# Half of each grouped-query pair's maxima one stretch earlier, in a two-layer hybrid attention kernel

## Chip, cores and metric

One core of one Trainium2 chip runs the whole kernel. The metric is the time of one execution in device microseconds (us). TensorE (PE in the profile) does the matmuls, with its weight loads listed apart (PEld); VectorE (DVE), ScalarE (ACT) and GpSimd (POOL) do the elementwise work; SyncE (SP) issues the transfers. TensorE writes its results to PSUM.

## What is computed

Two layers over 1024 latent tokens with 256 context tokens in front. In each layer one projection feeds three groups of heads: six heads of neighbourhood attention (a window of 8 x 16 grid positions and all context keys, with a learned bias), a bidirectional gated linear attention, and six query heads of grouped-query attention over all 1280 keys. Then an output projection, a residual with layer norm, and a gated feed-forward layer. The two softmax attentions are what the change touches:

```
# neighbourhood: scores of the window with a bias, and of the context, in one softmax
s_lat = q_r @ k_s * scale + bias          # outside the window: -inf
s_ctx = q_r @ k_ctx * scale
p = softmax(concat([s_lat, s_ctx]))
# grouped query: all latent and context keys in one softmax
s = q_blk @ keys * d ** -0.5
o = softmax(s) @ vals
```

Layer 0 also computes the outputs of the context tokens (10 blocks of 128 queries); the last layer needs only the latent ones (8 blocks).

## The kernel before

**Pairs and two stages.** Heads are worked on in pairs, two heads side by side in 64 rows each. `PAIRS = (0, 3, 1, 4, 2, 5)`: pairs 0, 1, 2 are neighbourhood pairs, 3, 4, 5 grouped-query pairs. Each pair has two stages. The first (`stage_a`: `na_a`, `ga_a`) finds the largest score of each query, which the softmax subtracts. The second (`stage_b`: `na_b`, `ga_b`) computes the scores again, keys by queries, with the maximum subtracted inside the matmul; then the exponential (ScalarE), the products with the values (TensorE, L950 and L1011) and the sums of the exponentials (GpSimd, L1046 and L1006). The text calls the first stage a pair's **maxima** and the time of a pair's second stage its **stretch**; the six stretches of a layer follow each other in the order of `PAIRS`.

**The maxima.** In `ga_a` (L923) each step is one matmul per head of a 128-query block against 512 or 256 keys (`raw_scores`, L483, tile `gs`) into a two-bank PSUM tile with tag "m", of which there is one buffer, and a VectorE reduction of that tile (L934, into tile `m`). A block of latent queries takes three steps (512, 512, 256 keys), a context block one. In `na_a` (L899) a block takes a step for the context keys (tile `sctx`, reduced at L907) and one for the window (tile `slat`, with two bias-and-maximum instructions, L917), through the same "m" buffer. At the end `max_rows` (L445) transposes the maxima by matmuls (tile `nmT`, L458). With that last part, a grouped-query pair has 27 steps in layer 0 and 25 in the last layer, a neighbourhood pair 19 and 17.

**The second stages.** `ga_b` has 39 places at which it pauses: a block of scores (L475, tile `sT`, two buffers, L945) or a value product (`weigh`, tile `gav`), in turn. `na_b` has 22 places: four blocks of scores over the context keys, their value products (tile `nav`), then eight groups of window scores, each with a bias addition on VectorE (L1023, tile `ptl`), the exponential, and a value product two groups later.

**What sets the order.** Everything is unrolled; each engine works through its own instructions in order. The loop at L1114 takes one place of the current pair's second stage, then some steps of the next pair's maxima, and so on. In a neighbourhood stretch the 27 (25) steps of the following grouped-query pair start after the second place and are spread evenly to the 19th, more than one and a half a place; in a grouped-query stretch the 19 (17) steps of the following neighbourhood pair start after the 12th place and run to the 36th. `in_turn` (L467) chains the matmuls of scores, raw scores and value products in just this written order, so TensorE runs them as written. Loads of a pair's keys, queries and biases are issued on SP's queue by `load` (L868), one pair ahead at least, and wait for free tiles in a pool of 31. The tails of the pair before (`tail`, L1066: normalisation, tile `rb`, through the same "m" buffer) use the first two or three places. The line that spreads the steps:

```
while done < min(na, na * (n - skip) // (places - 3 - skip)):
    next(a, 0)
    done += 1
```

Of the kernel before, what the change touches and what calls it, by code (L numbers as in the profile page):

```python
# [1 line left out]

# [50 lines left out]
def body(ctx: ExitStack, tc, xT, cT, w_ada, w_in, nbias, wa2, w_out, w_fi, w_fo, vecs, cc, consts, ropes, gmask, out):  # L53
# [18 lines left out]
    def slot(dt=F32, name="sl"):  # L72
        return slots.tile([P, NT], dt, tag="s", name=name)
# [239 lines left out]
    def run(g):  # L313
        for _ in g:
            pass
# [117 lines left out]
    def gate(ins, after):  # L433

        if after is not None:
            tc.add_manual_dep(ins.ins, after.ins.name, NOSYNC, reason="buffers in order of use")
        return ins
# [67 lines left out]
    PAIRS = (0, 3, 1, 4, 2, 5)  # L505
# [18 lines left out]
    for l in range(NL):  # L524
# [54 lines left out]
        NBQ = NG  # L579
        A = [slots.tile([P, 10, 2, 64], F32, tag="s", name=f"A{i}") for i in range(2)]  # L580

        def a_mm(p, ga, gb, xk_, X):

            ps = banks2(ps_s, "s", "aps")
            in_order([pe.matmul(ps[64 * c:64 * c + 64, hh, (g - ga) * 64:(g - ga + 1) * 64],
                                lhsT=xk_[32 * (2 * p + hh):32 * (2 * p + hh) + 32, P * g + 64 * c:P * g + 64 * c + 64],
                                rhs=X[32 * (2 * p + hh):32 * (2 * p + hh) + 32, P * g + 64 * c:P * g + 64 * c + 64],
                                start=True, stop=True)
                      for g in range(ga, gb) for c in range(2) for hh in range(2)])
            return (A[p][:, ga:gb].rearrange("p g h t -> p h g t"),  # L590
                    ps[:, :, :(gb - ga) * 64].rearrange("p h (g t) -> p h g t", t=64), gb - ga)

        abanks = [(p, g, min(g + 8, NG)) for g in range(0, NG, 8) for p in range(2)]
        for p, ga, gb in abanks:
            dst, src, n = a_mm(p, ga, gb, gk, gq)
# [6 lines left out]
        for lev in range(6):  # L602
# [8 lines left out]
            for p, ga, gb in abanks:  # L611
                dst, src, n = a_mm(p, ga, gb, xk_, X)
# [224 lines left out]
        def gla_split(pr):  # L837
            O = o_gl[pr]
            a, b = slot(F32R, "oh"), slot(F32R, "ol")
            oh_all[3 + pr], ol_all[3 + pr] = a, b  # L840

            def nat(t):
                return t[:, 0:SEQ].rearrange("p (g r c) -> p r g c", g=8, c=8)

            src = O[:, 0:SEQ].rearrange("p (r g c) -> p r g c", g=8, c=8)
            for r0 in (0, 8):
                sl = slice(r0, r0 + 8)
                act.copy(nat(a)[:, sl], src[:, sl])
                pool.tensor_tensor(out=nat(b)[:, sl], in0=src[:, sl], in1=f(nat(a)[:, sl]), op=ALU.subtract)
                yield  # L850
            if not last:
                act.copy(a[:, SEQ:NT], O[:, SEQ:NT])
                pool.tensor_tensor(out=b[:, SEQ:NT], in0=O[:, SEQ:NT], in1=f(a[:, SEQ:NT]), op=ALU.subtract)
# [5 lines left out]
        def opens(i):  # L859
            return last_b.get(PAIRS[max(0, PAIRS.index(i) - 2)]) if PAIRS.index(i) > 1 else None  # L860

        def load_hl(i, n, after, name):
            ts = [slot(F32R, f"{name}{a}") for a in "hl"]
            for a, t in enumerate(ts):
                gate(nc.sync.dma_start(f(t[:, :n]), sp[l][i][a, :, :n]), after)
            return ts

        def load(i):  # L868
            if i > 5 or i in loaded:
                return  # L870
            loaded.add(i)
            after = opens(i)
            if i < 3:
                kk = load_hl(S_NK + i, NT, after, "K")
                qq = load_hl(S_NQ + i, NQ, after, "Q")

                bs = [slot(F32, f"B{e}") for e in range(3)]
                for v in range(2):
                    for t, c, n, x in ((bs[v], 0, 384, 0), (bs[v], 768, 256, 384), (bs[2], 512 * v, 256, 640)):
                        gate(nc.sync.dma_start(t[:, c:c + 2 * n].rearrange("p (e n) -> p e n", e=2),  # L880
                                               nbias[l, 2 * i:2 * i + 2, v, :, x:x + n].rearrange("e p n -> p e n")), after)
            else:
                if not gkv:
                    gkv.extend(load_hl(S_GK, NT, after, "K"))
                kk, bs = gkv, None
                qq = load_hl(S_GQ + i - 3, NQ, after, "Q")
            heads[i] = [kk, qq, None, bs]
# [193 lines left out]
        def stage_a(i):  # L1081
            return (na_a if i < 3 else ga_a)(i)

        def stage_b(i):
            return (na_b if i < 3 else ga_b)(i)
# [25 lines left out]

        tails += [gla_split(pr) for pr in range(2)]
        sb = {"n": 0, "t": ps_s.tile([P, 2, 2, 512], F32, tag="s4", name="sT", bufs=1)}
        for x, i in enumerate(PAIRS):  # L1114
            nxt = PAIRS[x + 1] if x < 5 else None
            if nxt is not None:
                load(nxt)
            if i >= 3 and x < 4:
                load(PAIRS[x + 2])
            b, a = stage_b(i), stage_a(nxt) if nxt is not None else iter(())  # L1120
            live, tails = tails, []

            places, na, skip = (22, NBQ + 17, 2) if i < 3 else (39, NBQ + 9, 12)
            n = done = 0
            while next(b, 0) is None:
                live = [g for g in live if next(g, 0) is None]
                n += 1
# [3 lines that stand above are left out]
            run(a)  # L1131
            for g in live:
                run(g)
# [213 lines left out]
```

## Time and profile before

| | |
|---|---|
| median of 3 runs | 3759.79 us (3759.14 to 3766.27) |
| the profiled execution | 3766.09 us, span 3764.3 us |
| mean granted TensorE clock | 0.940 |
| TensorE matmuls, busy | 3468.6 us (92% of the span) |
| VectorE, ScalarE, GpSimd, busy | 1650.0, 920.1, 1240.3 us |
| grouped-query maxima: TensorE matmuls (L483, `gs`) | 300 instructions, 90.6 us |
| grouped-query maxima: VectorE reductions (L934) | 150 instructions, 154.7 us |

How to read it: a group's row gives its line, engine, operation, the tile that it writes and those that it reads, the shapes and the count; behind the first bar its busy time and the mean of one in nanoseconds; behind the second the idle time of its engine just before it and what ended most of that. In a row of the stage windows the first number after the stretch is its length, then for each engine the busy time and the number of instructions, and then the TensorE clock that was granted (1 is full speed), the busy share of the DMA engines and the bytes moved. A row of the timeline has the start, the duration of what is merged in the row, engine, line, operation, tiles, count, and in brackets the idle time before it with its releaser.

### The profile page before, as it was taken

The numbers are of one execution on the slowest core, as the hardware profiler recorded it, in microseconds if no ns is written. First come the engines' busy times: TensorE is split into PE (matmuls) and PEld (weight loads), VectorE is DVE, ScalarE is ACT, GpSimd is POOL, SyncE is SP. The second block draws the span as 40 slices with busy tenths as digits, with TensorE's granted clock in tenths as the row PEclk, the third lists the DMA queues.
The fourth block names the chain that finished last, engine by engine and source line by source line (L and its number), as shares of the span: only waits on it lengthen the run. The fifth ranks groups of instructions, "written<-read, shape, count | busy, mean of one in ns | idle before, by whom it ended". The sixth has DMA issues, their size and how long they took to land. (4 is left out here: it accounts for less than half of the span.)

```text
span 3764.3 us, 49308 instructions
## 1 busy us (share of the span) xinstructions
PE 3468.6 (92%) x20832; PEld 2557.0 (68%) x20832; DVE 1650.0 (44%) x2475; ACT 920.1 (24%) x1365; POOL 1240.3 (33%) x747
## 2 busy tenths in 40 slices
PE   6698988788999999999999869998879999999998
PEld 3587873333668888888876658774335688888875
DVE  2756554544354553554234553425553432222233
ACT  2213212233231111111113403223323321111123
POOL 1612314464272111111125551315443532222223
PEclk8699997898999999999999979998889999999999
DMA  5142340010321322222123212221102211111122
GB/s 171 48 150 77 114 152 24 7 56 9 126 70 45 97 80 70 77 91 65 36 71 98 70 58 72 71 96 43 56 1 86 63 40 50 51 51 46 51 70 84
DMA packets 287276, 262.93 MB, mean 70 GB/s; under 512 B 13840, under 2 KB 238416, under 8 KB 287056
## 3 DMA queue, kind: packets, MB, share of 16 engines
q1 hardware_dynamic: 287056, 259.80, 21.5%
q8 instruction: 163, 2.67, 0.3%
q14 instruction: 57, 0.47, 0.0%
HBM read 226.72 MB, written 33.03 MB: 69 GB/s over the span
## 5 line engine op out<-in xcount | busy, mean ns | idle before, releaser
L251 POOL TENSOR_TENSOR wlo<-wraw,whi 128x1024 fp32r<-128x1024 f32 (+3 forms) x228 | 502.2, 2204 | 1788.0 <-ACT whi L248 1726.3
L276 PE MATMUL mmps<-oh,whi 128*128 128x512 f32 (+2 forms) x2416 | 903.9, 375 | 7.2 <-ACT whi L248 7.2
L276 PE MATMUL mmps<-oh,wlo 128*128 128x512 f32 (+1 forms) x2416 | 902.4, 374 | 2.6 <-POOL wlo L251 2.6
L276 PE MATMUL mmps<-ol,whi 128*128 128x512 f32 (+1 forms) x2416 | 902.5, 374 | 1.9 <-DVE ol L230 1.9
L276 PEld LDWEIGHTS mmps<-oh,whi 128*128 128x128 f32 (+1 forms) x2416 | 457.2, 189 | 115.7 <-issue 19.9
L276 PEld LDWEIGHTS mmps<-oh,wlo 128*128 128x128 f32 x2416 | 456.8, 189 | 114.9 <-issue 25.5
L276 PEld LDWEIGHTS mmps<-ol,whi 128*128 128x128 f32 x2416 | 456.9, 189 | 97.3 <-issue 16.6
L248 ACT CAST whi<-wraw 128x1024 fp32r<-128x1024 f32 (+3 forms) x262 | 251.9, 962 | 967.8 <-PE mmps L276 912.0
L1192 DVE TENSOR_TENSOR sg<-mmps,sg 128x512 f32<-128x512 f32 (+1 forms) x110 | 70.1, 637 | 605.4 <-PE mmps L276 601.1
L276 PE MATMUL mmps<-hl,whi 128*128 128x512 f32 (+1 forms) x880 | 324.8, 370 | 1.0 <-DVE hl L1194 1.0
L276 PE MATMUL mmps<-hh,whi 128*128 128x512 f32 (+1 forms) x880 | 324.0, 371 | 0.0
L276 PE MATMUL mmps<-hh,wlo 128*128 128x512 f32 (+1 forms) x880 | 321.2, 369 | 0.0
L1161 DVE SCALAR_TENSOR_TENSOR z<-mmps,mod,z 128x512 f32<-128x512 f32 (+1 forms) x320 | 217.9, 694 | 198.6 <-PE mmps L276 197.8
L178 DVE SCALAR_TENSOR_TENSOR adacc<-adaw,scc,adacc 128x512 f32<-128x512 f32 x280 | 240.0, 900 | 89.2 <-DMA adaw<-in_w_ada_dram 88.8
L1046 POOL TENSOR_TENSOR gacc<-gacc,gpt 128x1024 f32<-128x1024 f32 x80 | 188.9, 2374 | 56.3 <-ACT gpt L1054 56.2
L934 DVE TENSOR_REDUCE m<-gs 128x2 f32<-128x1024 f32 (+1 forms) x150 | 154.7, 1031 | 115.0 <-PE gs L483 115.0
L276 PEld LDWEIGHTS mmps<-hh,whi 128*128 128x128 f32 x880 | 166.0, 189 | 41.3 <-issue 9.2
L276 PEld LDWEIGHTS mmps<-hh,wlo 128*128 128x128 f32 x880 | 165.6, 189 | 31.9 <-issue 2.5
L276 PEld LDWEIGHTS mmps<-hl,whi 128*128 128x128 f32 x880 | 166.1, 189 | 30.0 <-DVE hl L1194 1.2
L276 PE MATMUL mmps<-uh,whi 128*128 128x512 f32 (+3 forms) x408 | 156.1, 389 | 27.4 <-ACT uh L229 18.8
L483 PE MATMUL gs<-Kh,Qh 64*128 64x512 f32 (+1 forms) x300 | 90.6, 601 | 78.6 <-DVE m L934 75.3
L1054 ACT ACTIVATE gpt<-sT 128x1024 f32<-128x1024 f32 x120 | 122.8, 1024 | 146.9 <-PE sT L475 146.9
(238 smaller groups left out, 4761.7 us busy)
## 6 DMA issues: line engine op xcount, KB each, us to landing
wraw<-in_w_fi_dram SPq DMA_DIRECT2D x106, 512.0 KB, 3.9
adaw<-in_w_ada_dram SPq DMA_DIRECT2D x160, 256.0 KB, 3.5
wraw<-in_w_fo_dram SPq DMA_DIRECT2D x60, 384.0 KB, 3.1
wraw<-in_w_in_dram SPq DMA_DIRECT2D x40, 512.0 KB, 4.0
wraw<-in_w_out_dram SPq DMA_DIRECT2D x36, 512.0 KB, 3.6
sp<-sphi SPq DMA_DIRECT2D x40, 256.0 KB, 2.0
sp<-splo SPq DMA_DIRECT2D x40, 256.0 KB, 2.1
adaw<-in_w_ada_dram SPq DMA_DIRECT2D x16, 512.0 KB, 7.4
```

The source lines that it names most:

```text
L178: dve.scalar_tensor_tensor(out=a, in0=raw, scalar=scc[:, k, s_:s_ + 1], in1=a, op0=ALU.mult, op1=ALU.add)
L248: act.copy(a[:, :m], rw)
L251: (dve if pace["lo"] and pace["w"] % pace["lo"] == 0 else pool).tensor_tensor(out=b[:, :m], in0=rw, in1=f(a[:, :m]), op=ALU.subtract)
L276: ins = pe.matmul(o, lhsT=lhs, rhs=rhs, start=st, stop=(k == nk - 1 and lhs is b))
L483: inss = [pe.matmul(ps[:, e, :n], lhsT=Qh[rows(e), q0:q0 + P], rhs=Kh[rows(e), k0:k0 + n], start=True, stop=True) for e in range(2)]
L934: dve.tensor_reduce(out=m3[:, j, :, c], in_=ps[:, :, :n], axis=AX.X, op=ALU.max)
L1046: (dve if q and i == 5 else pool).tensor_tensor(out=acc[q], in0=prev if kb == 1 else acc[q], in1=pt, op=ALU.add)
L1054: act.activation(pt, ps, AF.Exp)
L1161: dve.scalar_tensor_tensor(out=zz, in0=ps[:, :n], scalar=g[:, m + c, s:s + 1], in1=zz, op0=ALU.mult, op1=ALU.add)
L1192: dve.tensor_tensor(out=sg[:, sl], in0=ps[:, :n], in1=sg[:, sl], op=ALU.mult)
```

## The change

The maxima of pairs 4 and 5 are cut in two. Their first half (13 of 27 steps in layer 0, 12 of 25 in the last layer) moves into the grouped-query stretch before: that of pair 3 for pair 4, and that of pair 4 for pair 5. There, half a grouped-query pair's maxima come first and the next neighbourhood pair's whole maxima behind them, together 32 (29) steps, spread from the fifth place to the 36th at about one a place. The second half stays in the neighbourhood stretch, 14 (13) steps spread over the same places as before. The first neighbourhood stretch keeps all 27 (25) steps of pair 3, since no grouped-query stretch is ahead of it, and the last stretch has no maxima, as before. The queries of pairs 4 and 5 are loaded one stretch earlier. No instruction is added or taken out.

```
+        steps_a = [NBQ + 9] * 3 + [NBQ + 17] * 3
+        maxima = {i: stage_a(i) for i in PAIRS[1:]}
+
+        def some(i, n):
+            for _ in range(n if n is not None else steps_a[i]):
+                next(maxima[i], 0)
+                yield
+            if n is None:
+                run(maxima[i])
+
         for x, i in enumerate(PAIRS):
-            nxt = PAIRS[x + 1] if x < 5 else None
-            if nxt is not None:
-                load(nxt)
-            if i >= 3 and x < 4:
-                load(PAIRS[x + 2])
-            b, a = stage_b(i), stage_a(nxt) if nxt is not None else iter(())
+            if x < 5:
+                load(PAIRS[x + 1])
+            if x in (0, 2):
+                load(PAIRS[x + 3])
+
+            half = steps_a[3] // 2
+            a, na, places, skip = (
+                (some(PAIRS[1], None), steps_a[3], 22, 2), (), (some(PAIRS[3], None), steps_a[3] - half, 22, 2), (),
+                (some(PAIRS[5], None), steps_a[3] - half, 22, 2), (iter(()), 0, 39, 0))[x] or (
+                chain(some(PAIRS[x + 2], half), some(PAIRS[x + 1], None)), half + steps_a[0], 39, 3)
             live, tails = tails, []
-
-            places, na, skip = (22, NBQ + 17, 2) if i < 3 else (39, NBQ + 9, 12)
+            b = stage_b(i)
```

More of the change, by code (lines that the diff above doesn't have):

```diff
@@ L1 @@
 from contextlib import ExitStack
+from itertools import chain
 import concourse.bass as bass
```

## The prediction

> **What bounds the kernel now.** I read the page's groups first, for the two that the change moves; then the busy time by stretch (the stage windows), the waits of TensorE inside one stretch, and the timeline instruction by instruction. The profiled execution took 3766.09 us, 1.8 us more than its span and 6.3 us above the median of the three runs (3759.79 us, 3759.14 to 3766.27). I count every term from the profiled execution and take the sum off the median.
>
> ```profile
> span 3764.3 us, 49308 instructions
> L934 DVE TENSOR_REDUCE m<-gs 128x2 f32<-128x1024 f32 (+1 forms) x150 | 154.7, 1031 | 115.0 <-PE gs L483 115.0
> L483 PE MATMUL gs<-Kh,Qh 64*128 64x512 f32 (+1 forms) x300 | 90.6, 601 | 78.6 <-DVE m L934 75.3
> ```
>
> 150 grouped-query maxima cost TensorE 90.6 us of matmuls and 75.3 us of waiting, because both sides wait for each other: the scores go into one PSUM buffer, VectorE reduces it, and the next scores need it back. The stage windows show where that counts. The first four rows are the four neighbourhood stretches that the change touches (two of each layer), from their first maximum to their last value product; the fifth is a grouped-query stretch with neighbourhood maxima, the sixth the last stretch, with no maxima. The last two rows are 13.7 us inside a neighbourhood stretch and 24.3 us inside a grouped-query stretch.
>
> ```profile
> core 0: us, PE busy (x) PEld busy (x) DVE busy (x) ACT busy (x) POOL busy (x), PEclk, DMA share, GB/s
> 701.10:753.20 52.10, 37.89 (x214) 19.42 (x214) 34.55 (x41) 8.33 (x12) 19.25 (x21) 0.71 0.04 15
> 830.60:883.00 52.40, 38.16 (x212) 19.23 (x212) 34.48 (x41) 8.32 (x12) 19.14 (x21) 0.71 0.00 1
> 2652.50:2700.60 48.10, 36.17 (x208) 18.41 (x208) 33.00 (x40) 8.51 (x11) 17.78 (x19) 0.75 0.06 18
> 2771.20:2820.30 49.10, 37.16 (x209) 18.68 (x210) 33.06 (x39) 8.55 (x11) 18.40 (x20) 0.72 0.00 1
> 760.90:817.60 56.70, 51.97 (x360) 23.22 (x358) 22.08 (x50) 23.57 (x26) 45.95 (x22) 1.00 0.11 39
> 890.80:941.00 50.20, 47.44 (x263) 18.68 (x261) 15.07 (x15) 23.34 (x25) 27.07 (x14) 1.00 0.06 16
> 701.10:714.80 13.70, 8.76 (x42) 3.11 (x44) 8.74 (x8) 1.44 (x3) 5.92 (x6) 1.00 0.00 0
> 782.60:806.90 24.30, 21.21 (x126) 9.33 (x126) 13.05 (x31) 8.70 (x9) 20.23 (x9) 1.00 0.00 1
> ```
>
> TensorE is busy 73% in the neighbourhood stretches and 92 to 95% in the other two. The maxima alone, in the same windows (columns: TensorE, weight loads, VectorE), and the waits of TensorE in those two:
>
> ```profile
> 701.10:753.20 52.10, 15.21 (x52) 6.50 (x52) 26.48 (x26) 0.71 0.04 15
> 2652.50:2700.60 48.10, 14.28 (x48) 5.66 (x48) 25.09 (x24) 0.75 0.06 18
> ```
> ```profile
> PE gs L483 <- DVE m L934: 14.0, 15, 2.0
> PE gs L483 <- DVE m L934: 11.6, 17, 1.3
> ```
>
> So 14.0 of the 14.2 idle microseconds of the first window end with a reduction. Neither engine is full: the single buffer's round trip is the bound, and since attention's matmuls are issued in one written order, whatever stands behind a waiting score matmul waits as well.
>
> **The change, step by step.** *The round trip.* Timeline rows of one neighbourhood stretch at full clock, then two at half clock (the same matmul at 0.79 instead of 0.50 us):
>
> ```profile
> 701.13 0.50 PE L483 MATMUL gs<-Kh,Qh 64*128 64x512 f32 x2 [0.52 <-DVE o L1077]
> 701.56 1.08 PE L950 MATMUL nav<-ptc,Va 128*64 128x512 f32 x4
> 702.95 0.50 PE L483 MATMUL gs<-Kh,Qh 64*128 64x512 f32 x2 [0.31 <-DVE m L934]
> 704.77 0.39 PE L483 MATMUL gs<-Kh,Qh 64*128 64x256 f32 x2 [1.32 <-DVE m L934]
> 705.00 0.39 PE L475 MATMUL sT<-Qh,Kh 64*128 64x512 f32 x2
> 705.95 0.50 PE L483 MATMUL gs<-Kh,Qh 64*128 64x512 f32 x2
> ...
> 715.82 0.79 PE L483 MATMUL gs<-Kh,Qh 64*128 64x512 f32 x2
> 718.04 0.80 PE L483 MATMUL gs<-Kh,Qh 64*128 64x512 f32 x2 [1.42 <-DVE m L934]
> ```
>
> A maximum over 512 keys holds the buffer 1.82 us (701.13 to 702.95, and again to 704.77), whether a value product stood between or nothing; one over 256 holds it 1.18 us (704.77 to 705.95). The first stretch of layer 0 in the list has 16 wide and 10 narrow ones: 16 x 1.82 + 10 x 1.18 = 40.9 us. VectorE's other work there is 34.55 - 26.48 = 8.1 us and falls between the reductions. 49.0 us; the window has 52.1, so 3.1 us are its end, after the last maximum. The model fits before, so I use it for after.
>
> *Removed from each of the four stretches.* In layer 0 the first 13 of 27 steps go (9 wide, 4 narrow); 7 wide and 6 narrow stay: 7 x 1.82 + 6 x 1.18 = 19.8, plus 8.1 and 3.1, is 31.0 us. The other limit, TensorE's own work at the clock it had, is 37.89 - 13/26 x 15.21 = 30.3 us. Two places in the middle get no maximum now, and their matmuls (about 1 us together by the 1.08 us value product) are no longer under a round trip: 32 us, so 20 less than 52.1. In layer 1 (16 wide, 8 narrow; 38.6 + 7.9 = 46.5 of 48.1 us) half goes: 19.3 + 7.9 + 1.6 = 28.8; TensorE's limit is 36.17 - 14.28/2 = 29.0; I take 30.6, 17.5 less. For four stretches: 2 x 20 + 2 x 17.5 = 75 us. What is late next there is TensorE itself, and then GpSimd: its sums took 19.25 us of the window, well under 32.
>
> *Added to each of the four grouped-query stretches.* The trace has no grouped-query maximum there. The nearest rows are a unit (one block of scores and one value product, two places) without maxima, and one with a maximum at each of its places:
>
> ```profile
> 771.26 0.51 PE L475 MATMUL sT<-Qh,Kh 64*128 64x512 f32 x2
> ...
> 773.63 0.50 PE L475 MATMUL sT<-Qh,Kh 64*128 64x512 f32 x2 [0.16 <-ACT gpt L1054]
> ...
> 786.83 0.39 PE L483 MATMUL sctx<-Kh,Qh 64*128 64x256 f32 x2 [0.50 <-DVE mx L917]
> ...
> 789.94 0.39 PE L483 MATMUL sctx<-Kh,Qh 64*128 64x256 f32 x2 [0.49 <-DVE mx L917]
> ...
> 812.22 1.20 PE L458 MATMUL nmT<-cst,nm 128*32 128x128 f32 x32
> ...
> 815.49 1.08 PE L458 MATMUL nmT<-cst,nm 128*32 128x128 f32 x32
> ```
>
> A unit takes 2.37 us bare and 3.11 us with two neighbourhood steps. With grouped-query steps in every place, three of them (1.82 + 1.82 + 1.18 = 4.82 us of buffer) spread over one and a half units (3.56 us): +1.26 us, and about 0.15 more where a narrow one is followed by a block of scores, which is longer than its round trip. Layer 0: four such groups and one wide step, 4 x 1.41 + 0.63 = 6.3 us; layer 1: four groups, 5.6 us. Lower end: only their matmuls, 9 x 0.43 (701.13 to 701.56) + 4 x 0.23 (704.77 to 705.00) = 4.8 us; upper end: as much as they cost where they were, 20 us. I take the round trip, since VectorE is free here (22.08 of 56.70 us). The wait that it adds stands on TensorE; behind it are the next block of scores or value product, then ScalarE's exponentials and GpSimd's sums, and all of them get the longer unit. The 19 neighbourhood steps behind them now stand in 19 places instead of 24: eight dense units cost 8 x 0.74 = 5.9 and two lone steps about 0.4; before, the whole lot cost 56.70 - 50.20 = 6.5 with 2.3 of transposes in it, so 4.2. That is +2.1 at most, 0 at least; the two edge blocks have narrower steps, I take +1.3. Together 7.6 and 6.9 us, 29 us for four stretches.
>
> *Loads.* The query tiles of the half-done pair are requested a stretch earlier and pass the next pair's keys and biases on SP's queue. Rows of the queue and of landing times:
>
> ```profile
> 620.03 0.34 SPq L865 DMA_DIRECT2D Qh<-sp  x1
> 620.42 0.94 SPq L880 DMA_DIRECT2D B<-in_nbias_dram  x2
> 621.45 0.41 SPq L865 DMA_DIRECT2D Ql<-sp  x1
> ```
> ```profile
> B<-in_nbias_dram SPq DMA_DIRECT2D x12, 384.0 KB, 9.2
> Ql<-sp SPq DMA_DIRECT2D x6, 640.0 KB, 8.6
> ```
>
> Even if they go out only at 620, as the buffers of the pair before came free, 8.6 us lets them land by 630, and the first moved maximum stands behind four places of the next stretch; the biases behind them are needed at the 18th place now, not the 14th. Nothing; up to 4 us a stretch if that cover is gone. GpSimd's queue is not passed. The order of the kernel's first and last stretch is unchanged.
>
> **Sum:** 75 - 29 = 46 us less: 3766.1 to 3720 for a like execution, 3759.8 to 3714 as median.
>
> **A rule against it.** The 701.10 to 714.80 row, 64% busy, runs at full clock, yet at 715.82 the same matmul takes 0.79 us, and the stretch's granted clock is 0.71: the longest wait in it was 2.0 us. The Trainium skill ("TensorE: Matmul & The Clock Gate", section "The HAM clock gate") halves the clock after an idle window of about 3.4 us, which would leave these stretches at full clock; the trace disagrees. Its section "A second HAM failure mode: psum-queue depth-cycling" has short idles at PSUM buffers make the clock swing, and with this the trace agrees. By that section the grouped-query stretches could begin to swing too; that is the third rival.
>
> **Rivals.**
> *Waits halve instead of vanishing.* Half the maxima take half of their matmuls and half of their waits along: (15.21 + 14.0)/2 = 14.6 and (14.28 + 11.6)/2 = 12.9 us, 55 us for four, less 29: -26, 3734 us. For it: a reduction still queues behind an addition of VectorE (8.1 us). Against: the round-trip model gives the window before within 3.1 us.
> *More.* Denser matmuls keep the full clock in the neighbourhood stretches (granted 0.71 to 0.75), about 3 us more each, and the added steps hide down to their lower end, 1.5 us each: -64, 3696 us.
> *Slower: the clock halves in the grouped-query stretches.* The 32 dense places last 22 + 29 = 51 us with about 44 us of matmuls; at half clock (0.79 for 0.50; 1.5 over a mixture) 66 us, 15 more, four times: -46 + 60 = +14, 3774 us. It decides once three quarters of those places run halved. For it: row 701.10 to 714.80. Against: 782.60 to 806.90, as dense as what comes, is 87% busy at clock 1.00, and for the new places I work out 89% (three units of 2.37 - 0.16 and 2.2 of maxima in 9.9 us).
> *Nothing.* The moved steps cost their 20 and 17.5 us where they land, or the built order keeps them where they were: 3760 us. Against: 3.11 for 2.37 us shows overlap.
>
> **Numbers.** Forecast 0.60 (3700 to 3726), waits halve 0.20, more 0.10, slower 0.05, nothing 0.05. Range 3694 to 3740: from the second rival's end to a little above the first's. A measurement of this kernel can tell about 0.2% (7.5 us) from no change: faster 0.90, within 0.05, slower 0.05.
>
> **What would show it.** In the changed profile: the four neighbourhood windows at 30 to 34 us with TensorE's wait for VectorE below 5 us; grouped-query stretches 7 us longer, granted clock still 1.00, a wide maximum every 1.8 us in their fifth to 17th places; the first stretch of each layer unchanged. Wrong if the neighbourhood windows stay above 38 us, if score matmuls in the grouped-query stretches take 0.6 us instead of 0.4, or if they lengthen by over 12 us.

## The result and the profile after

The change made the kernel faster: 3701.94 us as the median of four runs (3697.95 to 3703.34) beside 3761.0 us for four runs of the kernel before (3759.14 to 3766.27). The ratio is 0.9839, with a 95% interval of 0.9822 to 0.9856. The medians differ by 59.1 us, where 46 were forecast. The profiled execution of the changed kernel took 3701.86 us, 0.1 us from its median; that of before lay 5.1 us above its own, so the spans differ by 64.2 us.

The lines of the changed kernel have moved by one: L935 is the reduction of a grouped-query maximum, L484 its matmul, L476 the block of scores. From the page and the groups of the changed kernel:

```profile
span 3700.1 us, 49312 instructions
L935 DVE TENSOR_REDUCE m<-gs 128x2 f32<-128x1024 f32 (+1 forms) x150 | 154.8, 1032 | 107.6 <-PE gs L484 107.6
L484 PE MATMUL gs<-Kh,Qh 64*128 64x512 f32 (+1 forms) x300 | 76.1, 504 | 55.2 <-DVE m L935 49.2 <-DVE o L1078 5.3
```

The reductions are the same 150 at the same 1032 ns. Their matmuls fell from 90.6 to 76.1 us with the count unchanged, since each became shorter (601 to 504 ns), and TensorE's wait for the reductions fell from 75.3 to 49.2 us. The stage windows of the changed kernel show where. The columns are those of the prediction's rows; first the four neighbourhood stretches from the first maximum to the last value product, then the two grouped-query stretches of layer 0 that take in the moved steps:

```profile
702.60:731.80 29.20, 23.65 (x216) 12.42 (x218) 20.77 (x28) 8.82 (x12) 18.89 (x21) 1.00 0.30 107
816.00:846.80 30.80, 25.78 (x216) 13.76 (x216) 20.85 (x28) 8.82 (x12) 18.91 (x21) 0.89 0.00 1
2625.90:2656.00 30.10, 26.07 (x214) 13.88 (x216) 20.09 (x27) 9.02 (x13) 17.97 (x20) 0.89 0.05 15
2729.60:2758.10 28.50, 23.50 (x214) 12.44 (x215) 19.98 (x27) 9.04 (x12) 17.99 (x20) 1.00 0.00 1
624.20:688.30 64.10, 56.04 (x384) 25.47 (x382) 35.78 (x63) 23.51 (x26) 45.70 (x22) 1.00 0.06 22
737.70:801.80 64.10, 56.03 (x384) 25.51 (x382) 35.72 (x63) 23.57 (x26) 45.71 (x22) 1.00 0.00 1
```

The four neighbourhood windows together fell from 201.7 to 118.6 us, and their granted clock, 0.71 to 0.75 before, is now 0.89 to 1.00. TensorE's waits, in the first neighbourhood window and then in the first grouped-query window:

```profile
PE gs L484 <- DVE m L935: 3.3, 7, 1.0
PE sT L476 <- DVE ptl L1024: 1.4, 2, 0.9
```
```profile
PE sctx L484 <- DVE mx L918: 4.1, 8, 0.6
PE gs L484 <- DVE m L935: 2.8, 8, 0.4
```

The 14.0 us of waiting in the neighbourhood stretch became 3.3, the longest 1.0 us, and the moved maxima wait only 2.8 us in their new place. How that comes about is seen in the timeline of TensorE there (idle time before a row in brackets):

```profile
632.84 0.50 PE L484 MATMUL gs<-Kh,Qh 64*128 64x512 f32 x2 [0.52 <-DVE o L1078]
633.18 0.39 PE L476 MATMUL sT<-Qh,Kh 64*128 64x512 f32 x2
...
634.66 0.49 PE L484 MATMUL gs<-Kh,Qh 64*128 64x512 f32 x2 [0.39 <-DVE m L935]
635.09 1.08 PE L951 MATMUL gav<-gpt,Va 128*64 128x512 f32 x4
636.48 0.39 PE L484 MATMUL gs<-Kh,Qh 64*128 64x256 f32 x2 [0.32 <-DVE m L935]
...
637.66 0.49 PE L484 MATMUL gs<-Kh,Qh 64*128 64x512 f32 x2
...
654.22 0.38 PE L484 MATMUL sctx<-Kh,Qh 64*128 64x256 f32 x2 [0.39 <-DVE m L935]
```

The buffer goes round as before, 1.82 us for a wide maximum (632.84 to 634.66 to 636.48) and 1.18 for a narrow one (636.48 to 637.66). But a block of scores or a value product now stands under each of them, and what is left to wait is 0.3 to 0.4 us. A whole stretch is counted below from one final output copy to the next. First the kernel before, pair 3's stretch and the neighbourhood stretch behind it, then the same two after:

```profile
624.04:688.14 64.10, 57.80 (x446) 26.23 (x448) 24.54 (x52) 27.51 (x34) 47.52 (x24) 1.00 0.04 14
688.14:753.27 65.13, 48.95 (x310) 24.45 (x312) 40.55 (x49) 16.31 (x23) 23.40 (x24) 0.76 0.03 13
```
```profile
616.57:688.77 72.20, 62.29 (x472) 28.53 (x474) 38.21 (x65) 27.50 (x33) 47.76 (x24) 1.00 0.07 26
688.77:731.81 43.04, 35.51 (x316) 17.70 (x318) 26.77 (x36) 16.85 (x25) 23.85 (x25) 1.00 0.20 73
```

So pair 3's stretch grew by 8.1 us and the next shrank by 22.1. All four pairs of stretches: the neighbourhood ones went from 248.1 to 167.0 us (22.1, 20.9, 17.8 and 20.4 less), the grouped-query ones from 246.6 to 270.2 (8.1, 6.1, 6.6 and 2.8 more), together 57.5 us less. The rest of the 64.2: 7.5 up to the end of layer 0's first stretch, 3.2 in the last stretches of the two layers, 0.5 behind the last, and 4.5 more between the two layers' attentions, where no matmul was moved.

The 3.2 us are no gain of their own. A grouped-query pair's maxima end with transposes (tile `nmT`), and 32 of these matmuls ran behind the final output copy before and run ahead of it now. TensorE's count in layer 0's last stretch shows it, first before, then after:

```profile
883.16:941.07 57.91, 53.30 (x349) 21.69 (x350) 17.52 (x17) 27.26 (x32) 28.74 (x16) 1.00 0.05 14
846.84:902.96 56.12, 52.21 (x317) 20.88 (x318) 17.52 (x17) 26.67 (x31) 28.37 (x15) 1.00 0.05 14
```

In the same way each of the four neighbourhood stretches now holds 32 transposes more than before (48 became 80 in layer 0), and pair 4's stretches hold 32 fewer. By the two last stretches such a group is worth 1.8 and 1.4 us. Pair 3's stretches hold as many as before, so their 8.1 and 6.6 us are the added time as it is. The terms of 7.5, 0.5 and 4.5 us lie where the edit moves no matmul.

### The profile page after: what moved, and what is told of

Read it like the earlier page. It is cut to its first block, busy times and chain, and to the rows that moved or that the text cites. A ratio compares the mean times of both kernels' runs of the same rounds, so it can differ in the third digit from the quotient of the medians.

```text
span 3700.1 us, 49312 instructions
## 1 busy us (share of the span) xinstructions
PE 3423.4 (93%) x20832; PEld 2536.6 (69%) x20832; DVE 1634.0 (44%) x2475; ACT 920.2 (25%) x1365; POOL 1243.6 (34%) x747
## 4 chain that ended last, share of the span: by engine, by line
PE 81%; DVE 11%; ACT 4%; issue 2%; POOL 2%; DMA 1%; SPq 0%; ACTq 0%; DVEq 0%; POOLq 0%
PE mmps L277 60%; PE sT L476 4%; PE vps L656 3%; DVE m L935 3%; PE fs L358 2%; PE gav L951 2%; PE gs L484 2%; DVE S L735 1%; ACT gpt L1055 1%; DVE ut L229 1%; DVE slat L918 1%; PE nmT L459 1%; DVE ptl L1024 1%; PE spr L429 1%; PE adaps L185 1%
## 5 line engine op out<-in xcount | busy, mean ns | idle before, releaser
L935 DVE TENSOR_REDUCE m<-gs 128x2 f32<-128x1024 f32 (+1 forms) x150 | 154.8, 1032 | 107.6 <-PE gs L484 107.6
L277 PEld LDWEIGHTS mmps<-hl,whi 128*128 128x128 f32 x880 | 166.2, 189 | 30.1 <-DVE hl L1209 1.2
L1209 DVE TENSOR_TENSOR hl<-sg,hh 128x512 fp32r<-128x512 f32 (+1 forms) x110 | 128.7, 1170 | 67.1 <-ACT hh L1208 67.1
```

What stands on the lines that cost most here:

```text
L277: ins = pe.matmul(o, lhsT=lhs, rhs=rhs, start=st, stop=(k == nk - 1 and lhs is b))
L935: dve.tensor_reduce(out=m3[:, j, :, c], in_=ps[:, :, :n], axis=AX.X, op=ALU.max)
L1209: dve.tensor_tensor(out=b_[:, sl], in0=sg[:, sl], in1=f(a_[:, sl]), op=ALU.subtract)
```

## The experiments

The theory: a grouped-query maximum costs what the round trip of its one PSUM buffer leaves uncovered; there is little cover in a neighbourhood stretch at more than one step a place, and much in a grouped-query stretch at about one. Rivals: the earlier loads give the gain; the clock is the cause, and shorter waits only follow from it; and fewer steps count, not how densely they stand. Ratios are to the kernel before, with 95% intervals. Stretches are given in the order pair 1 and 2 of layer 0, then of the last layer (grouped-query ones: pair 3 and 4).

**The loads alone**, in the kernel before:

```
-            if i >= 3 and x < 4:
-                load(PAIRS[x + 2])
+            if x in (0, 2):
+                load(PAIRS[x + 3])
```

> The kernel before with only the earlier loads of the change (queries of pairs 4 and 5 one stretch earlier); no maximum is moved. Theory (the round trip through the single PSUM buffer is what the change relieves): the kernel before's time within its noise, 3753 to 3769 us, neighbourhood windows still 48 to 52 us. Rival (the loads were late and their earlier start gives part of the gain): 3720 to 3745 us.

Measured: 3761.04 us, ratio 1.0005 (0.9996 to 1.0015). The earlier loads give nothing and cost nothing.

**The half that stays, bunched.** In the changed kernel the 14 remaining steps of pairs 4 and 5 are spread to the 11th place instead of the 19th:

```
-                (some(PAIRS[1], None), steps_a[3], 22, 2), (), (some(PAIRS[3], None), steps_a[3] - half, 22, 2), (),
-                (some(PAIRS[5], None), steps_a[3] - half, 22, 2), (iter(()), 0, 39, 0))[x] or (
+                (some(PAIRS[1], None), steps_a[3], 22, 2), (), (some(PAIRS[3], None), steps_a[3] - half, 14, 2), (),
+                (some(PAIRS[5], None), steps_a[3] - half, 14, 2), (iter(()), 0, 39, 0))[x] or (
```

> The changed kernel, but the half of the maxima that stays in a neighbourhood stretch is packed at the old density (about 1.6 a place, third to 11th place) instead of 0.8 a place. Same work, same places in the grouped-query stretches. Theory (what costs is maxima standing closer than a round trip of 1.82 or 1.18 us): 13 round trips cover 9 places whose own matmuls take about 8 us, and the rest runs bare behind them: windows 33 to 35 us instead of 28.5 to 31, 15 to 22 us slower than the changed kernel, 3717 to 3724 us. Rival (only the number of maxima in the stretch counts): as the changed kernel, 3698 to 3706 us.

Measured: 3718.27 us, ratio 0.9891 (0.9874 to 0.9907). The stage window of the first neighbourhood stretch of this kernel, to be read beside the 43.04 of the changed one:

```profile
689.20:736.79 47.59, 38.21 (x332) 18.75 (x334) 26.25 (x36) 17.08 (x25) 23.52 (x24) 0.96 0.12 43
```

The four neighbourhood stretches took 47.6, 47.6, 44.2 and 45.5 us, 17.9 more than in the changed kernel, and the grouped-query ones the same within 0.5. The same number of steps, closer together, gives back a good quarter of the gain. With the same work on VectorE and TensorE, density counts, and not only the number.

**A third, two thirds, all.** Three kernels change one number of the changed kernel, how many of the 27 (25) steps are moved:

```
-            half = steps_a[3] // 2
+            half = steps_a[3] // 3
```

(and `2 * steps_a[3] // 3`, and `steps_a[3] - 1`).

> The changed kernel with 9 of 27 (8 of 25) steps moved instead of 13 (12). Round-trip theory: four steps more in each neighbourhood stretch at 1.6 us, four less in each grouped-query stretch at about 0.5 us: 4 to 5 us a pair of stretches, 15 to 25 us slower than the changed kernel: 3717 to 3727 us. With the clock on top (the neighbourhood windows fall back to 0.8 or less): up to 3735 us. Rival (the first few moved steps do it, density does not matter): 3700 to 3708 us.

> The changed kernel with 18 of 27 (16 of 25) steps moved instead of 13 (12). Theory: the grouped-query stretches then have more steps than places, so each further one pays nearly its whole round trip there (1.6 us on average, +5 us a stretch), while the neighbourhood windows only fall towards TensorE's and GpSimd's own work (29 to about 25.5 us): 3 to 10 us slower than the changed kernel, 3705 to 3712 us. Rival (each moved step gains as the first 50 did, 59 us by 50): about 20 us faster, 3680 us.

> The changed kernel with all 26 (24) maxima of pairs 4 and 5 moved, only the closing transposes stay. Theory: 45 steps in 33 places, every one pays its round trip: 16 x 1.82 + 10 x 1.18 = 41 us and 29 us for the neighbourhood pair's, 70 us where it was 51; the neighbourhood stretch falls only to its own work (24 us): 10 to 14 us slower a pair of stretches, 3740 to 3760 us. Rival (moved steps gain as the first half did): 3640 to 3660 us.

Measured: 3706.55 us (0.985, 0.9835 to 0.9865) for a third, 3704.79 (0.9851, 0.9835 to 0.9868) for two thirds, 3764.24 (1.0005, 0.9996 to 1.0014) for all. Whole stretches, pair 3's and the one behind it, first with a third, then with two thirds, then with all:

```profile
619.12:687.04 67.92, 60.17 (x464) 27.72 (x466) 33.84 (x61) 27.48 (x33) 47.76 (x24) 1.00 0.08 28
687.04:733.38 46.34, 38.89 (x292) 18.75 (x294) 30.88 (x40) 16.21 (x23) 23.48 (x24) 0.93 0.06 20
```
```profile
620.42:697.83 77.41, 64.67 (x450) 29.27 (x452) 42.57 (x70) 26.79 (x32) 47.72 (x24) 0.98 0.05 17
697.83:739.79 41.96, 36.14 (x338) 18.69 (x340) 22.79 (x31) 17.43 (x25) 23.88 (x25) 0.96 0.17 62
```
```profile
618.66:711.87 93.21, 73.53 (x466) 33.04 (x468) 50.38 (x81) 26.79 (x33) 47.46 (x24) 0.91 0.04 14
711.87:751.52 39.65, 33.30 (x338) 16.93 (x340) 13.38 (x20) 17.81 (x26) 23.52 (x24) 1.00 0.18 65
```

Together with the rows of before and after this gives the price of a step in both places. Where closing transposes cross the end of a stretch between two rows, the second figure takes that out; it is an estimate, at 1.4 to 1.8 us for 32 of them:

| steps in pair 3's stretch (33 places; before, 24) | its length, us | each added step | steps left in pair 1's stretch (17 places) | its length, us | each step taken out |
|---|---|---|---|---|---|
| 19 (before) | 64.10 | | 27 | 65.13 | |
| 28 | 67.92 | 0.42 | 18 | 46.34 | 2.09 |
| 32 (after) | 72.20 | 1.07 | 14 | 43.04 | 0.83; 1.2 to 1.3 |
| 37 | 77.41 | 1.04; 1.3 to 1.4 | 9 | 41.96 | 0.22; 0.5 to 0.6 |
| 45 | 93.21 | 1.98 | 1 | 39.65 | 0.29; 0.4 |

A step taken out of the neighbourhood stretch is worth the most until there is about one a place left; a step added to the grouped-query stretch costs little while there are places to spare and as much as a whole round trip beyond one a place. In the last layer, between a third and a half, each of the four steps still brought 1.71 and 1.10 us in its two neighbourhood stretches (47.30 and 43.25 to 40.46 and 38.84) and cost 0.60 and 0.70 (61.94 and 60.47 to 64.33 and 63.28); no transposes cross there. This fits the half's median, 4.6 us below the third's, though the intervals of the two overlap. With all moved, the waits are back, on the other side (TensorE's waits in 618.66 to 711.87 of that kernel):

```profile
PE gs L484 <- DVE m L935: 10.1, 15, 1.3
```

The expectation for a third failed: priced at the same rate a step, it should have kept much less of the gain than it did. Its time lies in the rival's range (3700 to 3708), and the rival is right that the first steps do most; that density doesn't matter is refuted by the bunched half. Two thirds came out at the edge of what was expected (3705 to 3712), all a little above it (3740 to 3760).

**The maximum buffer cut in two.** In the kernel before, the two-bank buffer of tag "m" becomes two one-bank buffers, one for each head, reduced and given back separately:

```
     def bank_m(name):
-        return banks2(ps_m, "m", name)[:, 0]
+        return ps_m.tile([P, 512], F32, tag="m", name=name, bufs=2)
...
-                    ps = banks2(ps_m, "m", "gs")
+                    ps = [bank_m("gs") for _ in range(2)]
                     raw_scores(ps, n, Qh, j * P, Kh, c0)
-                    dve.tensor_reduce(out=m3[:, j, :, c], in_=ps[:, :, :n], axis=AX.X, op=ALU.max)
+                    for e in range(2):
+                        dve.tensor_reduce(out=m3[:, j, e, c:c + 1], in_=ps[e][:, :n], axis=AX.X, op=ALU.max)
```

The neighbourhood maxima (`sctx`, `slat`) are split in the same way, and the other users of the buffer (transposes, sums, normalisation) get two one-bank buffers as well.

> The kernel before, schedule untouched, with the two-bank buffer cut into two buffers of one bank: each head's scores go to a tile of their own and are reduced by an instruction of their own, so the next scores can start when the first head's tile is free. VectorE gets one more reduction a step. Theory (single buffer's round trip): a wide maximum costs two reductions of about 0.69 us instead of 1.82 us, so neighbourhood windows fall by 6 to 10 us each, six of them, and the grouped-query stretches by 2: 3690 to 3725 us. Rival (VectorE's time is the bound, not the round trip): the extra reductions add about 0.15 us each, 25 us slower or more, 3785 us.

Measured: 3732.8 us, ratio 0.9927 (0.9912 to 0.9941): faster, so the rival, by which VectorE's own time is the bound, fell; but the gain was short of what was expected. The neighbourhood stretches took 61.6, 62.0, 55.6 and 56.1 us, 12.8 less together, although 96 closing transposes more fall into them than in the kernel before. TensorE's waits in the first of them, its window, and two rows of its timeline:

```profile
PE gs L483 <- DVE m L936: 6.2, 11, 1.3
```
```profile
673.65:735.20 61.55, 52.98 (x322) 28.00 (x324) 42.10 (x75) 16.28 (x23) 24.16 (x25) 0.78 0.06 22
```
```profile
687.94 0.38 PE L483 MATMUL gs<-Kh,Qh 64*128 64x256 f32 x1 [0.34 <-DVE m L936]
688.54 0.39 PE L483 MATMUL gs<-Kh,Qh 64*128 64x256 f32 x1 [0.22 <-DVE m L936]
```

The wait did shrink, from 14.0 to 6.2 us, but TensorE's busy time grew by 4.0 us, and the 52 matmuls of the maxima took 22.16 us there instead of 15.21. The two heads' matmuls of a narrow step, one row of "x2" and 0.39 us in the prediction's rows, here run one behind the other, 0.60 us apart. The clock hardly moved (0.78). In these stretches the shorter wait was worth a fifth of what the change brought there, with the transposes put right in both (about 17 beside 87 us): given back in part as TensorE time, and with hardly any clock won.

**The same split in the changed kernel:**

> The changed kernel with the buffer cut into two one-bank buffers, as in the run on the kernel before, which gained 27 us there. Theory (round trips still cost 7 us of waits in a grouped-query stretch and 3.3 us in a neighbourhood window of the changed kernel, and more in each layer's first stretch): 3 us less in each of four grouped-query stretches, 1 to 2 in each changed neighbourhood stretch, 4 in each first stretch: 3670 to 3690 us. Rival (the two cures work on the same wait, so nothing is left for the second): 3698 to 3706 us.

Measured: 3689.04 us, ratio 0.9803 (0.9787 to 0.982). The grouped-query stretches took 67.6, 67.5, 61.1 and 59.9 us, 14.1 less than in the changed kernel, the neighbourhood stretches 164.7 beside 167.0 us. Of the 23.6 us that the change added to the grouped-query stretches the split takes 14.1 away again. Some 2 to 3 of that are 48 transposes that now fall ahead of these stretches, by the price above. In the kernel before it had taken 4.3 there (246.6 to 242.3), which is no more than the 96 transposes that left them: there was next to nothing to win in them before the change.

**More work under the wait.** In the kernel before, each window-score block of a neighbourhood pair first runs two extra pairs of score matmuls, which the real ones overwrite:

```
+        for _ in range(again):
+            in_turn([pe.matmul(ps[:, e, :n], lhsT=Kh[rows(e), k0:k0 + P], rhs=Qh[rows(e), q0:q0 + n],
+                               start=True, stop=True) for e in range(2)])
...
-                last_b[i] = scores(ps, n, kk, g * P, qq, NM, j0 * P)
+                last_b[i] = scores(ps, n, kk, g * P, qq, NM, j0 * P, 2)
```

> The kernel before with TensorE kept busier in the neighbourhood stretches: ahead of each group's window scores two extra pairs of matmuls that the real ones overwrite (16 pairs a stretch, 5.4 us at full clock, 8.3 at half), outside the maxima's round trip. Theory of the clock (idle gaps let the clock halve, and this is a good part of the cost): the granted clock in these windows rises from 0.71 to 0.85 or more, and the added work is paid by faster matmuls: windows 50 to 54 us, 3745 to 3775 us. Rival (the clock is no cause, only the waits are): clock as before, windows longer by half of the added work or more, 3785 to 3800 us.

Measured: 3778.43 us, ratio 1.0044 (1.003 to 1.0058). The stretches grew to 68.8, 70.9, 60.5 and 61.3 us and the clock stayed at 0.74 to 0.80. The time lies in neither expected range, and the run doesn't decide: the filler was meant to make TensorE denser and so to raise the clock, but the stretch grew with it. The first stretch is 51.59 us busy of 68.80, 75%, as before (48.95 of 65.13).

**A short reduction.** In the kernel before, the reduction reads only the first 64 scores of a step, so that the rest of each maximum is left out; the exponentials are scaled to stay finite. No matmul is moved or removed.

```
-                    dve.tensor_reduce(out=m3[:, j, :, c], in_=ps[:, :, :n], axis=AX.X, op=ALU.max)
+                    dve.tensor_reduce(out=m3[:, j, :, c], in_=ps[:, :, :64], axis=AX.X, op=ALU.max)
```

> The kernel before, schedule and all matmuls untouched, with the grouped-query reductions cut short: each takes the maximum of the first 64 scores instead of 512 or 256 (and the exponentials are scaled by 0.01, so that they stay finite); the rest of the maximum is left out. A round trip falls from 1.82 and 1.18 us to about 0.9 and 0.8. Theory (round trips, with the halved clock as their consequence): the neighbourhood stretches fall by 12 to 17 us each, six of them, and run near full clock, with no matmul moved: 3665 to 3690 us. Rival (it is the amount of TensorE's work in these stretches, so that only moving it helps): 3740 to 3762 us.

Measured: 3678.2 us, ratio 0.9773 (0.9752 to 0.9794). The group of the reduction, the window of the first neighbourhood stretch, and TensorE's wait in it:

```profile
L934 DVE TENSOR_REDUCE m<-gs 128x2 f32<-128x128 f32 x150 | 43.5, 290 | 125.8 <-PE gs L483 125.8
```
```profile
669.66:717.10 47.44, 38.66 (x310) 19.11 (x312) 20.92 (x49) 16.33 (x24) 24.35 (x25) 1.00 0.06 21
```
```profile
PE gs L483 <- DVE m L934: 6.0, 11, 1.1
```

With all 27 steps still in it, the stretch took 47.44 us beside 65.13; the four took 193.9 beside 248.1, the grouped-query stretches stayed within 0.05 us of before, and the first stretch of layer 0 and the time between the layers shrank too, the maxima there being shorter. The four neighbourhood stretches fell by 17.7, 15.5, 10.5 and 10.6 us, two of them by less than the 12 to 17 expected. The same 310 matmuls took 38.66 us beside 48.95. Only VectorE's part of the round trip was shortened, and the clock rose from 0.76 to 1.00 (in the other three from 0.77, 0.79 and 0.77 to 0.93, 0.89 and 0.86): the lowered clock of before is no cause from outside, it follows from how these stretches run. This is the plainest test of the cause. What exactly the clock follows isn't shown: with the split buffer, TensorE's wait was as short (6.2 us in 11 waits), and the clock stayed at 0.78.

**Towards a faster kernel.** Three kernels combine the split with other numbers: the split and two thirds moved; the split and a third moved; and the split, half moved, and besides a third of pair 3's maxima moved ahead into the value projections before the first stretch, two steps a place, with its keys and queries loaded for that (pair 0's maxima, which were there already at one step a place, then stand at two as well). The core of the last one's edit:

```
+        early = steps_a[3] // 3
...
+            load(PAIRS[1], True)
             yield from stage_a(PAIRS[0])
+            for _ in range(early):
+                next(maxima[PAIRS[1]], 0)
+                yield
...
-        weave(units[6:], starts(), 3, 1)
+        weave(units[6:], starts(), 3, 2)
```

> The changed kernel with two one-bank buffers and 18 (16) steps moved instead of 13 (12). With one buffer this cost 3 us in all. Theory (a shorter round trip leaves room in the grouped-query stretches for more steps): 3680 to 3690 us, a little below the 3689 of 13 (12) steps. Rival (the places are full whatever the buffer): 3692 to 3700 us.

> The changed kernel with two one-bank buffers and 9 (8) steps moved. Theory: the neighbourhood stretches lose 2 to 3 us each, the grouped-query ones gain 1 to 2: 3689 to 3697 us. Rival (with two buffers the first stretch of nine already does all): 3684 to 3689 us.

> The changed kernel with two one-bank buffers, and 9 (8) steps of pair 3's maxima moved out of the first neighbourhood stretch of each layer, which the change leaves at 27 (25), into the value projections ahead of it, two steps a place; half the keys' and queries' tiles of pair 3 are loaded earlier, one bias tile later. Theory: the first stretches fall by 10 to 13 us as the others did from 27 to 18 steps, the projections pay 2 to 5: 3669 to 3680 us. Rival (the projections are dense, so the steps cost there what they gave): 3685 to 3700 us.

Measured: 3676.9 us (0.9778, 0.9762 to 0.9795), 3678.39 (0.9775, 0.9761 to 0.979) and 3675.77 (0.977, 0.9755 to 0.9784). All three beat the changed kernel, whose interval begins at 0.9822. Their own intervals overlap, so none of them is shown to be the best. The first and the second came out lower than either theory had them. All three also beat the split with a half (3689.04), mostly between the layers: from the end of layer 0's last stretch to the end of the next layer's first, that kernel took 1653.1 us, these 1641.8, 1643.4 and 1645.4. Why this part differs is open. What the early third is worth can be read in layer 0, beside the split with a half. The first stretch took 42.17 us instead of 57.79, but began 12.8 us later (570.51 instead of 557.76), where 2 to 5 us were expected to be paid. At its end 2.9 us are left, less than the 7.2 us by which that stretch differs between two kernels with the same order there (57.79 with a half, 64.98 with two thirds). So the last kernel's time lies in the theory's range, but not by its mechanism; in layer 0 the steps cost about what they gave, as the rival had it.

## Why the prediction was right, step by step

*What bounds it.* The round trip of the one buffer: shown. Shortening only VectorE's part of it, with no matmul moved, gives 54 us in the four neighbourhood stretches. That it isn't VectorE's time by itself shows in the bunched half and the split buffer: the first is 16 us slower than the change with the same VectorE work, the second 27 us faster than before with more of it.

*Removed from the neighbourhood stretches.* Forecast 75 us; the four windows lost 83.1, the four whole stretches 81.1, although each now holds 32 transposes more. The windows came to 29.2, 30.8, 30.1 and 28.5 us where 32 and 30.6 were forecast. The round-trip sums by themselves (31.0 and 28.8) make 119.6 us for the four, and 118.6 were measured; this closeness is partly luck, since with 7 waits, 3.3 us in all, the round trips no longer stood end to end in the first window. The mis-sized step is what was put on top of them, for places without cover and for TensorE's own limit, taken "at the clock it had": 30.3 us. The clock didn't stay, and in the first window TensorE was busy only 23.65 us. In the whole first stretch its busy time fell from 48.95 to 35.51 us, 13.4, although the transposes there grew by 1.2 (1.72 to 2.92 us). The moved matmuls account for 13/26 x 15.21 = 7.6 of it; the other 7.0 us, an estimate, are matmuls that are no longer stretched. So the forecast's second rival, with its "about 3 us more each" for a clock that holds, named the right mechanism for these stretches.

*Added to the grouped-query stretches.* Forecast 29 us, measured 23.6, but the stretches before and after aren't alike. Before, pair 4's stretch in the last layer took 60.44 us at a granted clock of 0.94, beside 57.66 at 1.00 with only the loads moved; and pair 4's two stretches have since lost 32 transposes each, 3.2 us by the two last stretches. With both put right the added time is about 29.5 us, an estimate. Pair 3's two stretches, which neither touches, grew by 8.1 and 6.6 us where 7.6 and 6.9 were forecast, so the step is right. In layer 0's first such stretch the moved steps go from 632.84 to 654.22, 21.4 us, where the prediction has six and a half bare units at 2.37 us and 6.3 added, 21.7.

*The total.* The spans differ by 64.2 us, 18.2 more than forecast. About 12 of that is the removed time, with the transposes put right (81.1 and 6.3, beside 75), and 2.8 that one stretch of the kernel before at 0.94. Another 3.5 (7.5 and 0.5 less 4.5) lie where nothing was moved, and that is luck.

*One linear price a step.* The prediction's 20 and 7.6 us are 1.5 us out and 0.6 in for each of 13 steps. That holds as a mean only: by the table, the first nine brought 2.09 and cost 0.42 each, the last four brought 1.2 to 1.3 and cost 1.07.

*Loads.* Nothing: shown by the loads alone (1.0005).

*The first stretch unchanged.* Its order was, its time wasn't. From the output copy before to its own, the kernel before and the changed kernel:

```profile
558.39:624.04 65.65, 49.50 (x238) 24.04 (x240) 34.54 (x41) 13.85 (x20) 25.24 (x26) 0.56 0.06 21
```
```profile
556.08:616.57 60.49, 42.84 (x238) 21.70 (x240) 34.47 (x41) 13.85 (x20) 25.23 (x26) 0.71 0.08 23
```

The same 238 matmuls took 6.66 us less, at a clock of 0.71 for 0.56, and the stretch 5.16 us less. Each microsecond by which matmuls are stretched cost 0.77 us of length there. The kernel with all steps moved, which has the same order there, took 0.57 over its last 58 us, so this isn't owed to the edit. If the same rate holds for the 7.0 us above, the clock's share of the first neighbourhood stretch's 22.1 us is about 5.4, an estimate; the rest is the moved matmuls and the waits.

*The rivals.* "Waits halve instead of vanishing" fell: 14.0 became 3.3 us, not 7. "Slower: the clock halves in the grouped-query stretches" didn't come with half of the steps (1.00), but began with all of them: 0.91, 0.96, 0.92 and 0.94, and by then the whole gain was gone. As for the Trainium skill's section "A second HAM failure mode: psum-queue depth-cycling" ("TensorE: Matmul & The Clock Gate"), by which short idles at PSUM buffers make the clock swing, the traces agree: waits that were at most 2.0 us long went with a clock of 0.76, and with 6.0 us of them in place of 14.0, after the short reduction, it was 1.00. The sum of the waits doesn't set it alone: 6.2 us with the split buffer went with 0.78.

*Left open.* How much of the gain is clock and how much is waiting isn't separated by a run: the filler was meant to, and failed. A second two-bank buffer, which leaves the two heads side by side, wasn't tried.

## What to carry to other kernels

Where one buffer goes back and forth between two engines, count its round trips against the places of other work that can stand under them: here a step cost 0.42 us while there were places to spare and 1.98 us beyond one a place, so spread such steps over all stretches that have places instead of emptying one. Price the first steps and the last ones moved separately; both curves bend near one step a place. When stretches are compared, check that the same instructions lie between their ends. When a bound of an engine is taken from a stretch at a lowered clock, work it out at full clock as well, because removing the waits can bring the clock back.

## What the runs showed of the hardware

- Splitting a two-bank score tile into two one-bank tiles cost TensorE part of its side-by-side pairs (a narrow step's two matmuls 0.60 us apart instead of 0.39 us for both): the 300 maxima matmuls took 125.3 us (38.4 idle before them) beside 90.6 (78.6), and 300 reductions of one head 164.8 us beside 154.7 for 150 of two.
- A reduction of 2 x 64 scores took 290 ns, where the mean over 2 x 512 and 2 x 256 was 1031.
- Being busy doesn't keep the clock up if it is counted in stretched matmuls: the stretch with the split buffer was 86% busy (52.98 of 61.55 us) at a clock of 0.78, while the one with short reductions held 1.00 at 81% (38.66 of 47.44). Waits of 6.2 and 6.0 us, 11 in each, went with these two clocks.
